# Differential attention: the four 32-row score products of two heads put into four PSUM banks

## The chip, the cores and the metric

The kernel runs on one core of a Trainium2 chip. The metric is the device time of one execution in microseconds (us): TensorE (PE) does the matrix products, VectorE (DVE) and ScalarE (ACT) the elementwise work, GpSimd (POOL) a little of it, and SyncE (SP) issues the weight loads.

## The reference, cut to what matters

Two layers of one transformer block are followed by two layers of another, over 512 tokens of width 1024. The second block's mixer has three attentions; the change lies in the first of these, differential attention with four heads of two 32-wide maps each:

```python
def diff_attention(q, k, v, lam):
    ...
        s = jnp.einsum('bhmqd,bhmkd->bhmqk', qblk, k).astype(jnp.float32) * scale
        qpos = bi * Q_BLOCK + jnp.arange(Q_BLOCK)
        s = jnp.where(kpos[None, :] <= qpos[:, None], s, -jnp.inf)
        p = jax.nn.softmax(s, axis=-1)
        a = p[:, :, 0] - lam * p[:, :, 1]
        return jnp.einsum('bhqk,bhkd->bhqd', a, vf)
```

Its output goes through a norm over each head's 64 values and, beside the outputs of the two other attentions, into the product with `w_out`.

## The kernel before

Every large product is split into three passes (`mm3`, L176 to L178) into one PSUM bank of tag `ps_mm`, of which there are three; a bank is free again when its reader has taken it. A weight comes by SP into a `wr` buffer, ACT casts it into a high part (L136, `wh`) and DVE subtracts that for the low part (L137, `wl`).

`mixers2` writes the second block's mixer in this order: forgetting attention; projections for differential attention; differential attention for the query tiles t = 3, 2, 1, 0 (at t, scores are 128 x 128(t+1) wide); projections `w_b2` with rotary embedding (`rope_proj`: three DVE operations L1064 to L1066, an addition on POOL L1067, transposes L1081, an ACT copy L1082) and `w_bv2`; then `to_feat` of the differential output (transposes L517), the dilated attention, and the product with `w_oa2`, whose first three of five input tiles come from the forgetting attention and whose last two from the differential one.

No one lays the instructions out by hand: `TileContext` with its scheduler sets the order on each engine, so products of a later line fill the time in which an earlier line's chain runs on DVE and ACT. Within an engine the order is then fixed, and an instruction that waits holds all behind it.

In differential attention one head goes like this. `score_pair` issues its two 32-row products into the two banks of tag `ps_S` (L1089; a 32-row product takes a quarter of the array's rows, and the first of a pair waits for the last read of the pair before, `sread`). `softmax_pair` takes each out with scale, mask and row minimum (DVE L1103) and exponentiates it (ACT L1105). Then the two maps are combined (DVE L1236 to L1240), and `pv` transposes the result in 128-wide pieces into one of the two banks of tag `ps_T` (L1115), copies it to SBUF (ACT L1117) and multiplies it with the values into `ps_o` (L1119). After four heads the tile is scaled (L1243), squared (L1246), summed (L1248), passed through a reciprocal root of eleven small DVE operations (L121 to L132) and scaled again (L1253). The dilated attention uses the same `softmax_pair` with 64-row products, two at a time.

Of the kernel before, what the change touches and what calls it, by code (L numbers as in the profile page):

```python
# [9 lines left out]
F32 = mybir.dt.float32  # L10
# [51 lines left out]
class Builder:  # L62
    def __init__(self, ctx, tc, d, out, cfg=None):
# [9 lines left out]
        self.pend, self.nstart, self.sread = [], 0, None  # L73
# [1010 lines left out]
    def score_pair(self, qk, ws):  # L1084

        nc = self.nc
        pts = [self.ps("S")[:, :ws] for _ in range(2)]
        for u, (q, k, row) in enumerate(qk):
            i = nc.tensor.matmul(pts[u], q, k, start=True, stop=True, tile_position=None if row is None else (row, 0))  # L1089
            if not u and self.sread is not None:  # L1090
                self.tc.add_manual_dep(i.ins, self.sread.name, SYNC, reason="pair")
        return pts

    def softmax_pair(self, mp, qk, t, in1s, scale):
# [5 lines left out]
        for pt, in1 in zip(pts, in1s):  # L1100
            s = mp.tile([P, S], F32, name="at_s", tag="at_s", bufs=5)[:, :w]
            st = mp.tile([P, 2], F32, name="at_st", tag="at_st", bufs=8)
            i = nc.vector.tensor_tensor_reduce(s, pt, in1, -scale, 3.0e38, ALU.add, ALU.min, accum_out=st[:, 0:1])  # L1103
            self.sread = i.ins
            nc.scalar.activation(s, s, AF.Exp, bias=st[:, 0:1], scale=-1.0, accum_out=st[:, 1:2])  # L1105
            out.append((s, st[:, 1:2]))
        return out

    def pv(self, mp, s, t, po, v):
# [7 lines left out]
        nc.scalar.copy(pT, tp[:, :w])  # L1117
# [39 lines left out]
    def mixers2(self, l, mp, act, nxt):  # L1157
# [69 lines left out]
        for t in reversed(range(NT)):  # L1227
# [3 lines left out]
            for h in range(4):  # L1231
                qt, kt = qka[h // 2], qka[2 + h // 2]
                rows = ((h % 2) * 64, (h % 2) * 64 + 32)
                (s0, d0), (s1, d1) = self.softmax_pair(mp, [(qt[b:b + 32], kt[b:b + 32], b) for b in rows], t, (msk, msk),
                                                       32 ** -0.5)
                nc.vector.reciprocal(den[:, h:h + 1], d0)  # L1236
                c = mp.tile([P, 1], F32, name="df_c", tag="df_c", bufs=4)
                nc.vector.reciprocal(c, d1)
                nc.vector.scalar_tensor_tensor(c, c, d0, lam[:, 2:3], ALU.mult, ALU.mult)
                nc.vector.scalar_tensor_tensor(s0, s1, c, s0, ALU.mult, ALU.add)  # L1240
                self.pv(mp, s0, t, po[:, h * 64:h * 64 + 64], lambda c: ya[c][:, h * 64:h * 64 + 64])
# [324 lines left out]
```

## Time and profile before

| | |
|---|---|
| time, median of 3 runs | 2783.43 us (2779.05 to 2784.21) |
| the profiled execution's own time | 2781.03 us |
| its span, first to last instruction | 2779.3 us |
| TensorE (PE) busy | 2701.2 us, 97% of the span |
| VectorE (DVE) busy | 1776.4 us, 64% |
| ScalarE (ACT) busy | 1181.6 us, 43% |
| chain that ended last | PE 77%, DVE 8%, DMA 8% |

The share of busy time is that of the whole span. The profile's chain runs back from the last instruction to what released each step. The two differential attentions lie at 1559 to 1632 us and 2230 to 2302 us of the span.

### The profile page before, as it was taken

To read this page: it belongs to the slowest core of one execution; us is meant where nothing else is said; L and a number is where in the kernel's file an instruction comes from. 1 tells how busy PE (TensorE), PEld (TensorE's weight loads), DVE (VectorE), ACT (ScalarE), POOL (GpSimd) and SP (SyncE) were. 2 spreads that over 40 slices of the span, in tenths; PEclk is the share of its full clock that TensorE was granted. 3 is DMA by queue.
4 is the path that set the end of the run, shared out by engine and by line. 5 is a ranking of instruction groups with operands and counts; after the bars stand their busy time and mean duration, and the time that the engine had idled before them with its cause. 6 is when DMAs were issued, how large, how long until landed. Compare 5 with 4: busy or idle time off the path is not lost.

```text
span 2779.3 us, 42737 instructions
## 1 busy us (share of the span) xinstructions
PE 2701.2 (97%) x16360; PEld 2305.9 (83%) x16360; DVE 1776.4 (64%) x3872; ACT 1181.6 (43%) x2340; POOL 250.6 (9%) x622
## 2 busy tenths in 40 slices
PE   8999999999999999999998999999999999999998
PEld 7887887889988788878987787888889787888887
DVE  7677777468676867765863666655554485664555
ACT  4644532326374543233543545333234554532332
POOL 2000100002200010000223200000001410100000
PEclk9999999999999999999999999999999999999999
DMA  4211487332221127743223221223332312133222
GB/s 155 75 41 62 131 267 230 107 106 92 88 75 44 59 82 245 257 151 106 99 72 104 52 68 65 83 89 97 102 94 86 99 39 84 49 105 97 89 86 78
DMA packets 87644, 285.59 MB, mean 103 GB/s; under 512 B 10972, under 2 KB 15132, under 8 KB 87440
## 3 DMA queue, kind: packets, MB, share of 16 engines
q1 hardware_dynamic: 81280, 266.49, 29.5%
q0 software_dynamic: 5872, 16.35, 2.2%
q8 instruction: 128, 2.10, 0.3%
q14 instruction: 76, 0.62, 0.1%
q10 hardware_dynamic: 288, 0.03, 0.0%
HBM read 280.69 MB, written 2.14 MB: 102 GB/s over the span
## 4 chain that ended last, share of the span: by engine, by line
PE 77%; DVE 8%; DMA 8%; ACT 3%; issue 2%; POOL 2%; SPq 0%; DVEq 0%; POOLq 0%; ACTq 0%
PE ps_mm L176 12%; PE ps_mm L177 12%; PE ps_mm L178 12%; DMA wm<-w_mod 6%; PE ps_T L176 5%; PE ps_T L178 5%; PE ps_T L177 5%; PE ps_S L176 5%; PE ps_S L178 5%; PE ps_S L177 5%; PE ps_S L1089 2%; DVE wm L1032 2%; PE ps_o L1135 1%; PE ps_T L1129 1%; PE ps_S L581 1%
## 5 line engine op out<-in xcount | busy, mean ns | idle before, releaser
L136 ACT CAST wh<-wr 128x1024 fp32r<-128x1024 f32 (+4 forms) x414 | 407.4, 987 | 677.4 <-PE ps_mm L177 225.8
L137 DVE TENSOR_TENSOR wl<-wr,wh 128x1024 fp32r<-128x1024 f32 (+4 forms) x414 | 472.5, 1142 | 305.0 <-ACT wh L136 297.8
L177 PE MATMUL ps_mm<-slotA,wh 128*128 128x512 f32 (+1 forms) x632 | 227.1, 362 | 3.4 <-DVE slotA L317 2.0
L176 PE MATMUL ps_mm<-slotA,wh 128*128 128x512 f32 (+1 forms) x632 | 226.2, 363 | 1.5 <-ACT slotA L316 0.7
L178 PE MATMUL ps_mm<-slotA,wl 128*128 128x512 f32 (+1 forms) x632 | 226.0, 359 | 0.0
L176 PE MATMUL ps_mm<-wh,slotA 128*128 128x256 f32 (+3 forms) x688 | 208.8, 304 | 0.0
L178 PE MATMUL ps_mm<-wh,slotA 128*128 128x256 f32 (+3 forms) x688 | 205.4, 299 | 0.0
L177 PE MATMUL ps_mm<-wl,slotA 128*128 128x256 f32 (+3 forms) x688 | 205.3, 299 | 0.0
L136 ACT CAST m_h<-tmp 128x512 fp32r<-128x512 f32 (+1 forms) x122 | 71.4, 587 | 209.2 <-DVE tmp L911 172.1
L1032 DVE CUSTOM_DVE_ANT_0 wm<-wm,sc 128x1024 f32<-128x1024 f32 x96 | 117.5, 1224 | 65.3 <-DMA wm<-w_mod 64.5
L176 PE MATMUL ps_mm<-slotB,wh 128*128 128x512 f32 (+1 forms) x408 | 142.5, 355 | 4.4 <-ACT slotB L136 3.6
L177 PE MATMUL ps_mm<-slotB,wh 128*128 128x512 f32 (+1 forms) x408 | 142.6, 350 | 1.4 <-DVE slotB L137 1.4
L176 PEld LDWEIGHTS ps_mm<-wh,slotA 128*128 128x128 f32 x688 | 131.6, 192 | 13.5 <-issue 10.6
L178 PE MATMUL ps_mm<-slotB,wl 128*128 128x512 f32 (+1 forms) x408 | 141.1, 346 | 0.0
L177 PEld LDWEIGHTS ps_mm<-slotA,wh 128*128 128x128 f32 x632 | 122.3, 194 | 22.3 <-DVE slotA L317 2.8
L176 PEld LDWEIGHTS ps_mm<-slotA,wh 128*128 128x128 f32 x632 | 121.3, 194 | 21.2 <-issue 3.0
L178 PEld LDWEIGHTS ps_mm<-slotA,wl 128*128 128x128 f32 x632 | 122.3, 193 | 18.2 <-issue 3.0
L178 PEld LDWEIGHTS ps_mm<-wh,slotA 128*128 128x128 f32 x688 | 131.2, 191 | 7.3 <-issue 6.6
L177 PEld LDWEIGHTS ps_mm<-wl,slotA 128*128 128x128 f32 x688 | 131.6, 191 | 5.2 <-issue 4.3
L176 PE MATMUL ps_S<-m_h,wh 128*128 128x512 f32 (+1 forms) x355 | 129.5, 365 | 3.2 <-DVE yacc L945 2.9
L178 PE MATMUL ps_S<-m_h,wl 128*128 128x512 f32 (+1 forms) x355 | 129.2, 364 | 0.0
L177 PE MATMUL ps_S<-m_l,wh 128*128 128x512 f32 (+1 forms) x355 | 129.2, 364 | 0.0
(635 smaller groups left out, 7177.4 us busy)
## 6 DMA issues: line engine op xcount, KB each, us to landing
wr<-w_up SPq DMA_DIRECT2D x152, 512.0 KB, 3.8
wm<-w_mod SPq DMA_DIRECT2D x96, 512.0 KB, 4.6
wr<-w_dn SPq DMA_DIRECT2D x64, 512.0 KB, 3.9
wr<-w_dn SPq DMA_DIRECT2D x32, 384.0 KB, 3.1
wr<-w_dn SPq DMA_DIRECT2D x32, 320.0 KB, 2.9
wr<-w_f SPq DMA_DIRECT2D x16, 512.0 KB, 3.8
wr<-w_pg SPq DMA_DIRECT2D x16, 512.0 KB, 3.7
wr<-w_t SPq DMA_DIRECT2D x12, 512.0 KB, 4.6
```

What stands on the lines that cost most here:

```text
L136: nc.scalar.copy(hi, src)
L137: nc.vector.tensor_tensor(lo, src, hi.bitcast(F32), ALU.subtract)
L176: nc.tensor.matmul(out, ah, bh, start=i == 0, stop=False)
L177: nc.tensor.matmul(out, ah, bl, start=False, stop=False)
L178: nc.tensor.matmul(out, al, bh, start=False, stop=i == n - 1)
L581: nc.tensor.matmul(pt, qs[f][b:b + 64, tt], qs[4][b:b + 64, k0:k0 + w], start=True, stop=True)
L1032: nc.vector.tensor_tensor_reduce(w, w, self.sc, 1.0, 0.0, ALU.mult, ALU.add, accum_out=self.mod[l][:, j:j + 1])
L1089: i = nc.tensor.matmul(pts[u], q, k, start=True, stop=True, tile_position=None if row is None else (row, 0))
L1129: nc.tensor.transpose(tp[:, c * P:c * P + P], s[:, c * P:c * P + P], self.ident)
L1135: nc.tensor.matmul(po[u * 64:u * 64 + 64], v(c, u), pT[:, c * P:c * P + P], start=c == 0, stop=c == t, tile_position=(0, u * 64))
```

## The change

The scores of two heads are asked for together: two products into the banks of `ps_S`, two into those of `ps_T`. The first of the four waits for the last reads of both kinds of bank (`sread`, and the new `tread`: the last eviction of a score from a `ps_T` bank or the last copy of transposed weights out of one). All four maps are then evicted and exponentiated, both heads are combined, and only then do the two heads' transposes and products with the values follow, written one after the other. Where a pair alone is asked for (the two other attentions), nothing changes.

```diff
     def score_pair(self, qk, ws):
...
-        pts = [self.ps("S")[:, :ws] for _ in range(2)]
+        pts = [self.ps(b)[:, :ws] for b in "SSTT"[:len(qk)]]
+        first = self.sread, self.tread if len(qk) > 2 else None
         for u, (q, k, row) in enumerate(qk):
             i = nc.tensor.matmul(pts[u], q, k, start=True, stop=True, tile_position=None if row is None else (row, 0))
-            if not u and self.sread is not None:
-                self.tc.add_manual_dep(i.ins, self.sread.name, SYNC, reason="pair")
+            for r in () if u else first:
+                if r is not None:
+                    self.tc.add_manual_dep(i.ins, r.name, SYNC, reason="pair")
         return pts
...
-            self.sread = i.ins
+            if n < 2:
+                self.sread = i.ins
+            else:
+                self.tread = i.ins
...
-        nc.scalar.copy(pT, tp[:, :w])
+        self.tread = nc.scalar.copy(pT, tp[:, :w]).ins
...
-            for h in range(4):
-                qt, kt = qka[h // 2], qka[2 + h // 2]
-                rows = ((h % 2) * 64, (h % 2) * 64 + 32)
-                (s0, d0), (s1, d1) = self.softmax_pair(mp, [(qt[b:b + 32], kt[b:b + 32], b) for b in rows], t, (msk, msk),
-                                                       32 ** -0.5)
...
-                self.pv(mp, s0, t, po[:, h * 64:h * 64 + 64], lambda c: ya[c][:, h * 64:h * 64 + 64])
+            for i in range(2):
+                qt, kt = qka[i], qka[2 + i]
+                four = self.softmax_pair(mp, [(qt[b:b + 32], kt[b:b + 32], b) for b in range(0, P, 32)], t, (msk,) * 4, 32 ** -0.5)
+                for h in (2 * i, 2 * i + 1):
+                    (s0, d0), (s1, d1) = four[h % 2 * 2:h % 2 * 2 + 2]
...
+                for h in (2 * i, 2 * i + 1):
+                    s0 = four[h % 2 * 2][0]
+                    self.pv(mp, s0, t, po[:, h * 64:h * 64 + 64], lambda c: ya[c][:, h * 64:h * 64 + 64])
```

The scheduler then lays out the instructions anew. On SP and POOL the order stays; on PE, DVE and ACT it differs in one stretch of each of the two layers, the same in both, and nowhere else. Every product that was there is there. In what follows `ps_S_15585` and the like are single banks' contents, and the line numbers of the changed kernel are 1 to 7 higher than those of the profile (L1090 is L1089, L1110 is L1105, L1120 is L1115, L1122 is L1117, L1124 is L1119, L1245 is L1240).

**First place: PE and ACT at t = 3, second half of the heads.** Before, the two products of a head (`ps_S`) stand together between passes of a `w_b2` projection:

```order
L176 MATMUL ps_mm_16107<-wh_16041,slotA_13688 128x256
L177 MATMUL ps_mm_16107<-wl_16042,slotA_13688 128x256
L1089 MATMUL ps_S_15585<-slotB_15103,slotB_15101 128x512
L1089 MATMUL ps_S_15586<-slotB_15103,slotB_15101 128x512
L178 MATMUL ps_mm_16107<-wh_16041,slotA_13689 128x256
```

Now one of the two `ps_T` products stands alone, right behind the transposes of the heads before (this stretch of PE's order), and the three others follow later, behind those heads' last product with the values (the next stretch):

```order
L1124 MATMUL ps_o_15527<-ya3_15403,at_pT_15568 128x64
L1120 MATMUL ps_T_15574<-ident_81,at_s_15545 128x128 x4
L1090 MATMUL ps_T_15587<-slotB_15103,slotB_15101 128x512
L176 MATMUL ps_mm_16193<-wh_16183,slotA_13680 128x256
L177 MATMUL ps_mm_16193<-wl_16184,slotA_13680 128x256
```

```order
L1124 MATMUL ps_o_15527<-ya3_15403,at_pT_15579 128x64
L1090 MATMUL ps_S_15585<-slotB_15103,slotB_15101 128x512
L1090 MATMUL ps_S_15586<-slotB_15103,slotB_15101 128x512
L1090 MATMUL ps_T_15588<-slotB_15103,slotB_15101 128x512
L1081 MATMUL ps_mm_16169<-ident_81,rp_a_16163 128x128
L1081 MATMUL ps_mm_16175<-ident_81,rp_a_16163 128x128
L176 MATMUL ps_mm_16193<-wh_16189,slotA_13692 128x256
```

The two products L1081 are the last transposes into two of the three `ps_mm` banks; six passes into the third follow, and the next pass needs the bank of `ps_mm_16169`. On ACT the copy that frees it (`slotB_16027`) stands, in the changed kernel, behind two of the four exponentials:

```order
L1122 COPY at_pT_15579<-ps_T_15574 128x512
L1110 ACTIVATE at_s_15593,at_st_15594<-at_s_15593,at_st_15594 128x512
L1110 ACTIVATE at_s_15597,at_st_15598<-at_s_15597,at_st_15598 128x512
L1082 COPY slotB_16027<-ps_mm_16169 128x512
L1082 COPY slotB_16028<-ps_mm_16175 128x512
L1110 ACTIVATE at_s_15601,at_st_15602<-at_s_15601,at_st_15602 128x512
L1110 ACTIVATE at_s_15605,at_st_15606<-at_s_15605,at_st_15606 128x512
```

What moved: the fourth product left the other three, and exponentials of 512 columns now stand ahead of the copy just after their scores were issued.

**Second place: DVE at t = 2, first half of the heads.** The names are `df_t`, `df_r` (the reciprocal root of the tile before), `rp_a`, `rp_b` (rotary embedding), `wl` (a weight's low part), `at_s` (the combined map). Before, the combination of the last head of that half stands so:

```order
L1064 TENSOR_TENSOR rp_a_16218<-ps_mm_16193,c_ropeb_14050 128x256
L1065 TENSOR_TENSOR rp_b_16219<-ps_mm_16193,c_ropeb_14050 128x4x32
L131 TENSOR_TENSOR df_t_15648<-df_t_15648,df_v_15647 128x4
L1066 TENSOR_TENSOR rp_b_16219<-ps_mm_16193,c_ropeb_14050 128x4x32
L1238 RECIPROCAL df_c_15731<-at_st_15727 128x1
L132 SCALAR_TENSOR_TENSOR df_r_15646<-df_t_15648,df_r_15646 128x4
L1239 SCALAR_TENSOR_TENSOR df_c_15731<-df_c_15731,at_st_15723,lam_15520 128x1
L130 TENSOR_TENSOR df_t_15648<-df_r_15646 128x4
L1240 SCALAR_TENSOR_TENSOR at_s_15722<-at_s_15726,df_c_15731,at_s_15722 128x384
```

Now a weight's low part of 768 columns stands just ahead of the combined map, and the rest of the rotary step behind it:

```order
L1243 RECIPROCAL df_c_15691<-at_st_15679 128x1
L130 TENSOR_TENSOR df_t_15648<-df_r_15646 128x4
L1244 SCALAR_TENSOR_TENSOR df_c_15691<-df_c_15691,at_st_15675,lam_15520 128x1
L1064 TENSOR_TENSOR rp_a_16311<-ps_mm_16286,c_ropeb_14050 128x256
L131 TENSOR_TENSOR df_t_15648<-df_t_15648,df_v_15647 128x4
L137 TENSOR_TENSOR wl_16484<-wr_16481,wh_16483 128x768
L1245 SCALAR_TENSOR_TENSOR at_s_15674<-at_s_15678,df_c_15691,at_s_15674 128x384
L1065 TENSOR_TENSOR rp_b_16312<-ps_mm_16286,c_ropeb_14050 128x4x32
L1066 TENSOR_TENSOR rp_b_16312<-ps_mm_16286,c_ropeb_14050 128x4x32
```

On PE the transposes of `at_s_15674` stand behind 14 passes of 256 columns and six L1081 that follow that group's scores; the next pass needs the bank `ps_mm_16286`, which the last of these rows frees.

**Third place: PE at the end, t = 0.** Before, passes of `w_bv2` stand around the last product with the values; 49 of them lie between it and the transposes L517 of the finished output:

```order
L177 MATMUL ps_mm_16531<-wl_16502,slotA_13694 128x384
L1119 MATMUL ps_o_15914<-ya0_15400,at_pT_16001 128x64
L178 MATMUL ps_mm_16531<-wh_16501,slotA_13695 128x384
L176 MATMUL ps_mm_16557<-wh_16483,slotA_13680 128x384
L177 MATMUL ps_mm_16557<-wl_16484,slotA_13680 128x384
```

Now these passes have all gone before, and so have 27 passes of `w_oa2` (nine into each of the three `ps_mm` banks, all that need no differential output); 16 of the 27 stand behind the scores of the first half of the heads at t = 0, and from there on no pass stands before L517. The order ends so (`ps_S_16663` and later are dilated attention):

```order
L1090 MATMUL ps_T_15963<-slotB_15103,slotB_15101 128x128
L1090 MATMUL ps_S_16663<-slotB_16030,slotB_16027 128x128
L1090 MATMUL ps_S_16664<-slotB_16030,slotB_16027 128x128
L1120 MATMUL ps_T_15994<-ident_81,at_s_15968 128x128
L1090 MATMUL ps_S_16687<-slotB_16031,slotB_16028 128x128
L1090 MATMUL ps_S_16688<-slotB_16031,slotB_16028 128x128
L1120 MATMUL ps_T_15999<-ident_81,at_s_15976 128x128
L1124 MATMUL ps_o_15914<-ya0_15400,at_pT_15996 128x64
L1090 MATMUL ps_S_16711<-slotB_16032,slotB_16029 128x128
L1090 MATMUL ps_S_16712<-slotB_16032,slotB_16029 128x128
L1124 MATMUL ps_o_15914<-ya0_15400,at_pT_16001 128x64
L517 MATMUL ps_T_16639<-ident_81,ya0_15400 128x128
```

What moved: the filler is spent before the last heads' chain begins, and the first three dilated score pairs moved into it.

## Rows read from the trace of the kernel before

**Rows 1.** The page's head: the span, then busy time, share of the span and instructions of each engine.
```profile
span 2779.3 us, 42737 instructions
PE 2701.2 (97%) x16360; PEld 2305.9 (83%) x16360; DVE 1776.4 (64%) x3872; ACT 1181.6 (43%) x2340; POOL 250.6 (9%) x622
```
**Rows 2.** Busy time by stretch, differential attention of the first and of the second layer of the block: from:to, length, then busy time (and instructions) of PE, PE's weight loads, DVE, ACT, POOL, the granted clock, DMA share and GB/s.
```profile
1559.00:1611.00 52.00, 52.00 (x392) 42.96 (x392) 43.22 (x167) 28.87 (x77) 8.30 (x10) 1.00 0.14 39
1611.00:1640.00 29.00, 29.00 (x201) 27.94 (x200) 18.14 (x88) 12.28 (x44) 2.75 (x3) 1.00 0.08 23
2230.00:2290.00 60.00, 60.00 (x462) 51.15 (x462) 51.01 (x210) 32.37 (x89) 9.63 (x11) 1.00 0.10 28
```
**Rows 3.** PE in order of time, four short stretches: start, length, engine, line, operation. A product counts as two instructions here, so x4 is a pair and x2 a single one. The last stretch is a single 64-row product of the dilated attention.
```profile
1568.34 0.28 PE L176 MATMUL ps_mm<-wh,slotA 128*128 128x256 f32 x1
1568.46 0.28 PE L177 MATMUL ps_mm<-wl,slotA 128*128 128x256 f32 x1
1568.67 1.13 PE L1089 MATMUL ps_S<-slotB 32*128 32x512 f32 x4
1569.73 0.38 PE L178 MATMUL ps_mm<-wh,slotA 128*128 128x256 f32 x1
...
1584.80 0.91 PE L1089 MATMUL ps_S<-slotB 32*128 32x384 f32 x4
1585.64 0.39 PE L177 MATMUL ps_mm<-wl,slotA 128*128 128x256 f32 x1
...
1600.38 0.70 PE L1089 MATMUL ps_S<-slotB 32*128 32x256 f32 x4
1601.02 0.39 PE L176 MATMUL ps_mm<-wh,slotA 128*128 128x256 f32 x1
...
1654.64 0.70 PE L1089 MATMUL ps_S<-slotB 64*128 64x256 f32 x2
1655.26 0.50 PE L178 MATMUL ps_mm<-slotA,wl 128*128 128x512 f32 x1
```
**Rows 4.** Groups of equal instructions between 1559 and 1640 us: busy us, mean ns of one, then the idle time before them and what ended it.
```profile
L1103 DVE CUSTOM_DVE_ANT_0 at_s<-ps_S,c_caus 128x384 f32<-128x384 f32 x8 | 4.3, 549 | 0.4 <-PE ps_S L1089 0.4
L1239 DVE SCALAR_TENSOR_TENSOR df_c<-df_c,at_st,lam 128x1 f32<-128x1 f32 x16 | 5.7, 354 | 0.3
L1064 DVE TENSOR_TENSOR rp_a<-ps_mm,c_ropeb 128x256 f32<-128x256 f32 x12 | 5.0, 416 | 0.0
L137 DVE TENSOR_TENSOR wl<-wr,wh 128x768 fp32r<-128x768 f32 x4 | 3.8, 950 | 0.0
L1082 ACT COPY slotB<-ps_mm 128x512 f32<-128x512 f32 x6 | 3.2, 589 | 2.6 <-PE ps_mm L1081 2.4
L1240 DVE SCALAR_TENSOR_TENSOR at_s<-at_s,df_c 128x384 f32<-128x384 f32 x4 | 2.5, 617 | 0.1
L131 DVE TENSOR_TENSOR df_t<-df_t,df_v 128x4 f32<-128x4 f32 x12 | 1.9, 156 | 0.2
L1243 DVE TENSOR_TENSOR ya<-ps_o,df_den 128x256 f32<-128x256 f32 x4 | 1.7, 422 | 8.3 <-PE ps_o L1119 8.3
L1248 DVE TENSOR_REDUCE df_ssq<-tmp 128x4 f32<-128x256 f32 x4 | 1.7, 416 | 0.6 <-ACT tmp L1246 0.6
```
**Rows 5.** ACT in order of time behind the first pair of scores at t = 3, which PE issues at 1559.51; in brackets the idle time before and what ended it.
```profile
1561.40 0.72 ACT L1105 ACTIVATE at_s<-at_s,at_st 128x512 f32<-128x512 f32 x1 [2.78 <-DVE at_st L1103]
1562.12 0.71 ACT L1105 ACTIVATE at_s<-at_s,at_st 128x512 f32<-128x512 f32 x1
1562.83 0.41 ACT L1131 COPY at_pT<-ps_T 128x128 f32<-128x128 f32 x2
```
**Rows 6.** From a pair of scores of t = 0 on PE to its combined map on DVE, in order of time (rows of both engines' timelines).
```profile
1613.10 0.49 PE L1089 MATMUL ps_S<-slotB 32*128 32x128 f32 x4
...
1615.97 0.35 DVE L1240 SCALAR_TENSOR_TENSOR at_s<-at_s,df_c 128x128 f32<-128x128 f32 x1
```
**Rows 7.** The end of differential attention, from DVE's, PE's and ACT's timelines: scaling of tile t = 0, its last scaling (four instructions), the transposes of the finished output, and their cast.
```profile
1631.95 0.42 DVE L1243 TENSOR_TENSOR ya<-ps_o,df_den 128x256 f32<-128x256 f32 x1 [6.92 <-PE ps_o L1119]
...
1635.64 0.87 DVE L1253 SCALAR_TENSOR_TENSOR ya<-ya,df_r,row 128x64 f32<-128x64 f32 x4
...
1640.34 1.04 PE L517 MATMUL ps_T<-ident,ya 128*128 128x128 f32 x8
...
1641.41 0.58 ACT L136 CAST slotA<-ps_T 128x512 fp32r<-128x512 f32 x1
...
1642.06 0.39 PE L177 MATMUL ps_mm<-slotA,wh 128*128 128x512 f32 x1
1642.29 0.39 PE L178 MATMUL ps_mm<-slotA,wl 128*128 128x512 f32 x1
```
**Rows 8.** PE's timeline where it had waited (in brackets how long), and busy time by stretch behind those waits, with the granted clock third from the end (columns as in rows 2).
```profile
1503.31 1.23 PE L1089 MATMUL ps_S<-slotB 64*128 64x512 f32 x2 [5.50 <-DVE at_st L1103]
...
1742.27 1.14 PE L266 MATMUL ps_mm<-n_dg,ones 128*128 128x256 f32 x2 [1.83 <-ACT n_dg L263]
...
1500.00:1507.00 7.00, 3.69 (x13) 2.18 (x14) 3.63 (x12) 3.01 (x8) 4.07 (x8) 0.51 0.42 150
...
1742.30:1745.80 3.50, 3.50 (x15) 3.32 (x16) 2.48 (x8) 2.02 (x5) 0.00 (x0) 0.51 0.01 2
```

More of the change, by code (lines that the diff above doesn't have):

```diff
@@ L72, in __init__ @@
         self.nmm, self.banks, self.late = 0, ("mm",), None
-        self.pend, self.nstart, self.sread = [], 0, None
+        self.pend, self.nstart, self.sread, self.tread = [], 0, None, None
         xa = cp.tile([P, NF * S], F32, name="x")
@@ L1099, in softmax_pair @@
         out = []
-        for pt, in1 in zip(pts, in1s):
+        for n, (pt, in1) in enumerate(zip(pts, in1s)):
             s = mp.tile([P, S], F32, name="at_s", tag="at_s", bufs=5)[:, :w]
@@ L1230, in mixers2 @@
             msk = self.c_caus[:, (3 - t) * P:]
-            for h in range(4):
-                qt, kt = qka[h // 2], qka[2 + h // 2]
-                rows = ((h % 2) * 64, (h % 2) * 64 + 32)
-                (s0, d0), (s1, d1) = self.softmax_pair(mp, [(qt[b:b + 32], kt[b:b + 32], b) for b in rows], t, (msk, msk),
-                                                       32 ** -0.5)
[L1236 to L1240, printed above, removed]
-                self.pv(mp, s0, t, po[:, h * 64:h * 64 + 64], lambda c: ya[c][:, h * 64:h * 64 + 64])
+            for i in range(2):
[3 more added lines that the diff above has]
+                    (s0, d0), (s1, d1) = four[h % 2 * 2:h % 2 * 2 + 2]
+                    nc.vector.reciprocal(den[:, h:h + 1], d0)
+                    c = mp.tile([P, 1], F32, name="df_c", tag="df_c", bufs=4)
+                    nc.vector.reciprocal(c, d1)
+                    nc.vector.scalar_tensor_tensor(c, c, d0, lam[:, 2:3], ALU.mult, ALU.mult)
+                    nc.vector.scalar_tensor_tensor(s0, s1, c, s0, ALU.mult, ALU.add)
+                for h in (2 * i, 2 * i + 1):
+                    s0 = four[h % 2 * 2][0]
+                    self.pv(mp, s0, t, po[:, h * 64:h * 64 + 64], lambda c: ya[c][:, h * 64:h * 64 + 64])
             o3 = ya[t].rearrange("p (h e) -> p h e", e=64)
```

## The prediction

> **What bounds the kernel now.** I began with the page's head: PE is busy in 97% of the span [rows 1], so a microsecond in which PE has nothing to do is probably a microsecond of the result. Then the busy time of the two stretches that the change reorders: PE is busy in all of 52.00 us, of 29.00 us and of 60.00 us, at the full clock, while DVE has 43.22 us of the first 52 [rows 2]. In this stage PE never waits; its filler, the passes of the next projections, covers every chain on DVE and ACT. So the change can gain only what it takes from PE's own work, and it loses whatever it uncovers. Last I read single instructions at the places where the order moved.
>
> **PE's own work.** From the start of a pair of 512-wide scores to the next instruction PE takes 1569.73 - 1568.67 = 1.06 us; at 384 it is 0.84, at 256 it is 0.64 [rows 3]. A single 64-row product of 256 columns takes 1655.26 - 1654.64 = 0.62 us [rows 3], as much as a pair: two products in different rows of the array run side by side, and one alone saves nothing. I call each such burst a unit. Before there are 16 units per layer. Four products issued together would make 8. But the new order does not issue four together. The third product waits only for its own `ps_T` bank, which comes free early; so it goes alone, and the three others follow, as the first place shows. That is again two units for two heads, and three for the first half at t = 3 (pair, one, one): 17 units, +1.06 us per layer. Against that, four fewer changes between passes and attention work (about 0.1 us each: between the pass at 1568.46 and the scores at 1568.67 lie 0.21 us instead of the 0.12 us between two passes [rows 3]) and one dilated unit of 0.62 us less, because its two products now stand together. I take **0** for PE's work. What three side by side cost no row shows; bounds are a pair (nothing more) and a pair and one more unit. I take the pair, because a pair costs the same as one.
>
> By the Trainium skill (TensorEngine Tiling (Array Packing), section Theoretical Speedup) a contraction of 32 rows or fewer can run up to four times as fast in row tiles. The pair rows agree for two, and no run here shows four; by it the 16 units would become 8, which is the second rival below.
>
> **The waits that the new order makes.** Two heads' chain is now one: four evictions, four exponentials, two combinations, and no next scores until the transposed copies have left the `ps_T` banks. I went through PE's order behind each group of scores and compared when PE arrives with when DVE and ACT are done. At most groups PE still arrives later. Three places are left in each layer.
>
> *First place (t = 3).* Behind the three scores PE has 1.06 us of scores, about 0.2 of transposes and six passes of 0.12 us [rows 3], so with changes of work it stands after 2.1 us before a pass whose bank is freed by the ACT copy. That copy comes behind two exponentials. Counted from the issue of the scores at 1559.51, the first exponential starts at 1561.40 and ACT is free for the next thing at 1562.83, 3.32 us later [rows 5]; with 0.59 us for the copy [rows 4] the bank is free at 3.9. **1.8 us.** Bounds: 0, since today such copies hold PE nowhere in this stage, and 2.5, if DVE is half a microsecond late with the evictions.
>
> *Second place (t = 2).* Scores 0.84, 14 passes of 0.12, six transposes of about 0.11 and changes of work: PE arrives after 3.35 us. DVE has from the same moment: scaling 0.42, four evictions of 0.55, sum 0.42, the rotary product 0.42, the weight's low part 0.95, the combination 0.35 and 0.62 and six small operations of about 0.16 [rows 4], together 6.3 us without a wait of its own. No filler is left, since two `ps_mm` banks wait for transposes and the third for the rotary step behind the combination. **3.0 us**; bounds 1.5 (means overlap by a tenth where operations follow each other) and 4.
>
> *Third place (the end).* After its scores for the first half at t = 0 PE has 16 passes of 512 columns, 0.23 us apart [rows 7], then only attention. From the end of those passes: transposes, copies and products of the first half until the last scores are issued, 1.5 us. From scores to a combined map a pair takes 1615.97 + 0.35 - 1613.10 = 3.2 us [rows 6]; the second combination adds 0.7, so 3.9. Transposes, a copy queued behind dilated exponentials, the product, and dilated work on DVE ahead of the scaling: 2.2. From scaling to the last scaling 1635.64 + 0.87 - 1631.95 = 4.6 us [rows 7], which today lies under the 8.4 us of passes up to L517 at 1640.34. Half the transposes and the cast of 0.58 us [rows 7]: 1.0. Together 13.2 us. In that time PE does some 4.0 us that it owes anyway (five units of 0.4, two of them the last scores, three dilated ones; eight transposes L517 of 1.0; the rest small). **9.2 us.** Bounds: 7, without the dilated work in between, and 12.
>
> *The clock.* After a wait of 5.50 us ended at 1503.31 the granted clock of the next microseconds was 0.51, the lower of its two levels (1.2 instead of 2.4 GHz); a wait of 1.83 us that ended at 1742.27 was followed by 3.50 us at 0.51 with PE busy throughout [rows 8]. Half speed for 3.5 us costs about 1.7 us. I take two such stretches per layer, behind the second and the third place: **3.4 us.** Bounds: one (1.7) and three (5.1).
>
> **The sum.** 1.8 + 3.0 + 9.2 + 3.4 + 0 = 17.4 us per layer, 34.8 for both. Against the profiled execution's own time: 2781.03 + 34.8 = 2815.8. That execution lies 2.4 us under the median of the runs shown, so I give **2818 us**. What follows the stage does not give it back: the passes spent early are the filler that is missing there later, and PE's total is the same.
>
> **The rivals.**
> 1. *Only the end waits* (slower, less). If DVE and ACT run further ahead of PE in the middle than my sums say, as they do today, the first two places vanish: 9.2 + 1.7 = 10.9, for two layers 21.8, about 2805; with the lower bound of the end 17.4, about 2801. For it: no wait of PE today in 141 us of this stage [rows 2]. Against: the bank at the second place is freed by an operation that stands behind 6 us of DVE work.
> 2. *Packing pays* (faster). If the lone product still runs beside its neighbours, or the four do meet, 8 units per layer fall away: 2 x (1.06 + 0.84 + 0.64 + 0.42) = 5.9 us, 11.8 for both layers, and if nothing waits the time is 2772. It decides at the moment the `ps_T` bank of the third product comes free: it would have to be no earlier than that of the fourth. Against it: in the order, transposes, products with the values or passes stand between the third and the other three in every group.
> 3. *Three do not pack.* If the third in a burst takes its own unit, seven bursts per layer add 1.06 + 2 x (0.84 + 0.64 + 0.42) = 4.9 us, 9.8 in all: 2828. For it: no row shows three. Against: one 64-row product costs what two cost.
> 4. *Nothing changes*: filler covers everything as today; then PE's work alone counts, 2781 to 2785. For it speaks the stage's record without a wait; against it the passes missing before L517.
>
> Another rule of the Trainium skill, on the same page (section PSUM Bottleneck), says that row packing speeds up TensorE but not the eviction of its banks. Had four met, the evictions behind them would still be what they are today, and the time would be that of the forecast less what rival 2 gains on PE; 43.22 us of DVE in 52 agree that there is little room.
>
> **How the numbers follow.** Forecast 0.56, rival 1 0.22, rival 3 0.12, rival 4 0.06, rival 2 0.04. The low end is rival 1 with the end at its lower bound, 2801, and I put it at 2800; the high end takes the upper bounds of the waits in both layers (12 + 4 + 2.5 + 5.1 = 23.6, 47.2 in all, 2831) or rival 3, and a little of both: 2836. A measurement of this kernel tells about 0.2% (5.6 us) from no change. Faster by more: rival 2, 0.04. Within: rival 4, 0.06. Slower by more: the rest, 0.90.
>
> **What would show it.** In the profile after, PE's row of the two stretches should fall under 100%: its timeline should show a wait at L176 ended by an ACT copy L1082 at t = 3, a wait at the transposes L1120 at t = 2 ended by DVE, and before L517 gaps that add up to some 9 us per layer, with a granted clock of 0.5 behind them. The scores should show as one product alone and three together, the three taking no longer than a pair. The forecast is wrong if PE stays busy in both stretches; if bursts of four appear; or if the waits are there and the time is not, because later waits shrank by as much.

## The result and the profile after

| | before | after |
|---|---|---|
| median of the runs | 2783.82 us (4 runs, 2779.05 to 2788.0) | 2820.38 us (4 runs, 2813.03 to 2823.0) |
| ratio | | 1.0133, 95% interval 1.0116 to 1.0149: slower by 1.2 to 1.5% |
| profiled execution, its span | 2781.03 us, 2779.3 us | 2818.74 us, 2817.0 us |

The forecast was 2818 us. Two of plan1's eleven executions took over 4000 us at a mean granted clock under 0.6 and are left out of its time below.

The head of the page after (span, then busy time and instructions of each engine), against [rows 1]:

```profile
span 2817.0 us, 42733 instructions
PE 2715.1 (96%) x16360; PEld 2313.3 (82%) x16360; DVE 1775.2 (63%) x3872; ACT 1180.3 (42%) x2340; POOL 250.3 (9%) x622
```

The span is 37.7 us longer, with 13.9 us more of busy PE although no product was added. To put both on a stage, I cut the trace at two products that stand in either kernel ahead of the second block's mixer and behind it (L266, which spreads a norm's factors), with the same 2048 instructions of PE between them. The two stretches before, one per layer (columns as in [rows 2]):

```profile
1440.98:1742.27 301.29, 289.71 (x2050) 243.25 (x2048) 173.71 (x559) 149.77 (x377) 54.39 (x106) 0.99 0.24 71
2110.81:2414.69 303.88, 290.96 (x2051) 245.50 (x2050) 172.86 (x556) 149.82 (x377) 54.34 (x106) 0.98 0.24 71
```

The same two after, then the five stretches of them in which the granted clock was at its lower level and was not before, then one stretch that was so before too:

```profile
1445.29:1763.69 318.40, 296.89 (x2051) 248.47 (x2049) 173.07 (x559) 149.40 (x377) 54.36 (x106) 0.97 0.23 68
2130.75:2452.82 322.07, 298.76 (x2050) 250.83 (x2049) 171.98 (x556) 149.16 (x377) 54.39 (x106) 0.95 0.22 67
...
1605.90:1609.30 3.40, 3.40 (x16) 3.40 (x17) 3.30 (x14) 0.58 (x2) 1.48 (x1) 0.50 0.66 175
1660.50:1670.70 10.20, 6.04 (x25) 4.62 (x26) 6.52 (x34) 3.87 (x15) 0.00 (x0) 0.50 0.00 0
2274.90:2278.30 3.40, 3.40 (x19) 3.40 (x18) 1.96 (x6) 0.67 (x2) 0.31 (x1) 0.50 0.02 5
2292.00:2295.40 3.40, 3.40 (x17) 3.36 (x16) 3.26 (x13) 0.48 (x1) 1.51 (x1) 0.50 0.72 209
2346.60:2356.80 10.20, 6.02 (x24) 4.74 (x25) 6.43 (x34) 3.76 (x13) 0.00 (x0) 0.50 0.00 0
...
1506.90:1513.70 6.80, 6.20 (x24) 4.69 (x25) 3.24 (x13) 3.55 (x9) 4.02 (x8) 0.50 0.44 134
```

The stage is 17.1 us longer in the first layer and 18.2 us in the second, 35.3 of the 37.7 us; the rest lies in unchanged code. Of these, length less busy PE, that is waiting, grew by 9.9 and 10.4 us, and busy PE by 7.2 and 7.8 us. Half of the busy time at 0.50 is what the clock cost: (3.40 + 6.04) / 2 = 4.7 and (3.40 + 3.40 + 6.02) / 2 = 6.4 us.

The largest of PE's waits after, between 1555 and 1672 us, where before there were none [rows 2]; the second layer has the same (us in total, times, longest):

```profile
PE ps_T L517 <- DVE ya L1260: 4.1, 1, 4.1
PE ps_T L1120 <- DVE at_s L1245: 3.3, 2, 2.2
PE ps_mm L176 <- ACT slotB L1082: 1.7, 1, 1.7
```

**First place.** PE's timeline at t = 3 after (a product counts as two instructions, so the first stretch is one product alone and the second three), to be held against [rows 3], and ACT's behind the same scores:

```profile
1581.35 1.12 PE L1090 MATMUL ps_T<-slotB 32*128 32x512 f32 x2
1582.40 0.38 PE L176 MATMUL ps_mm<-wh,slotA 128*128 128x256 f32 x1
...
1585.58 0.70 PE L1090 MATMUL ps_S<-slotB 32*128 32x512 f32 x2
1585.60 0.69 PE L1090 MATMUL ps_T<-slotB 32*128 32x512 f32 x1
1586.12 0.59 PE L1090 MATMUL ps_S<-slotB 32*128 32x512 f32 x2
1586.13 0.59 PE L1090 MATMUL ps_T<-slotB 32*128 32x512 f32 x1
1586.65 0.44 PE L1081 MATMUL ps_mm<-ident,rp_a 128*128 128x128 f32 x2
...
1589.52 0.39 PE L176 MATMUL ps_mm<-wh,slotA 128*128 128x256 f32 x1 [1.72 <-ACT slotB L1082]
```

```profile
1587.48 0.72 ACT L1110 ACTIVATE at_s<-at_s,at_st 128x512 f32<-128x512 f32 x1 [5.38 <-DVE at_st L1105]
...
1588.90 1.05 ACT L1082 COPY slotB<-ps_mm 128x512 f32<-128x512 f32 x2
```

The lone product takes 1582.40 - 1581.35 = 1.05 us, the three together 1586.65 - 1585.58 = 1.07: each a unit, like the pair of [rows 3]. Then PE stands 1.72 us before the bank whose copy ACT does behind two exponentials.

**Second place.** The scores at t = 2 and the transposes that wait, on PE, and on DVE the weight's low part ahead of the combined map:

```profile
1600.23 0.59 PE L1090 MATMUL ps_S<-slotB 32*128 32x384 f32 x2
...
1605.90 0.90 PE L1120 MATMUL ps_T<-ident,at_s 128*128 128x128 f32 x3 [2.23 <-DVE at_s L1245]
```

```profile
1604.37 0.95 DVE L137 TENSOR_TENSOR wl<-wr,wh 128x768 fp32r<-128x768 f32 x1
1605.23 0.61 DVE L1245 SCALAR_TENSOR_TENSOR at_s<-at_s,df_c 128x384 f32<-128x384 f32 x1
```

**Third place.** PE from the end of the passes (1655.95) to their resumption, and DVE's scaling and last scaling, against [rows 7]:

```profile
1655.95 0.38 PE L1120 MATMUL ps_T<-ident,at_s 128*128 128x128 f32 x2
...
1658.81 0.49 PE L1090 MATMUL ps_S<-slotB 64*128 64x128 f32 x4 [0.59 <-DVE at_st L1105]
1660.40 0.40 PE L1120 MATMUL ps_T<-ident,at_s 128*128 128x128 f32 x1 [1.10 <-DVE at_s L1245]
...
1663.03 0.69 PE L1124 MATMUL ps_o<-ya,at_pT 128*128 128x64 f32 x2
1667.83 1.97 PE L517 MATMUL ps_T<-ident,ya 128*128 128x128 f32 x8 [4.11 <-DVE ya L1260]
1669.62 1.49 PE L176 MATMUL ps_mm<-slotA,wh 128*128 128x512 f32 x3
```

```profile
1663.76 0.42 DVE L1250 TENSOR_TENSOR ya<-ps_o,df_den 128x256 f32<-128x256 f32 x1 [0.32 <-PE ps_o L1124]
...
1667.29 0.87 DVE L1260 SCALAR_TENSOR_TENSOR ya<-ya,df_r,row 128x64 f32<-128x64 f32 x4
```

From the end of the passes to the next pass are 1669.62 - 1655.95 = 13.7 us, the output's norm bare among them.

### The profile page after: what moved, and what is told of

The parts are those of the page before. It is cut to its first block, busy times and chain, and to the rows that moved or that the text cites. A ratio compares the mean times of both kernels' runs of the same rounds, so it can differ in the third digit from the quotient of the medians.

```text
span 2817.0 us, 42733 instructions
## 1 busy us (share of the span) xinstructions
PE 2715.1 (96%) x16360; PEld 2313.3 (82%) x16360; DVE 1775.2 (63%) x3872; ACT 1180.3 (42%) x2340; POOL 250.3 (9%) x622
## 4 chain that ended last, share of the span: by engine, by line
PE 76%; DVE 9%; DMA 8%; ACT 3%; issue 2%; POOL 2%; SPq 0%; DVEq 0%; POOLq 0%; ACTq 0%
PE ps_mm L176 12%; PE ps_mm L177 12%; PE ps_mm L178 12%; DMA wm<-w_mod 6%; PE ps_T L176 5%; PE ps_T L178 5%; PE ps_T L177 5%; PE ps_S L176 5%; PE ps_S L178 5%; PE ps_S L177 5%; PE ps_S L1090 2%; DVE wm L1032 2%; PE ps_o L1140 1%; DVE wl L137 1%; PE ps_T L1134 1%
## 5 line engine op out<-in xcount | busy, mean ns | idle before, releaser
L1110 ACT ACTIVATE at_s<-at_s,at_st 128x512 f32<-128x512 f32 (+3 forms) x160 | 89.1, 558 | 99.8 <-DVE at_st L1105 98.5
```

## The experiments

The changed kernel leaves open whether the chain of two heads is simply too long for the stage, or PE's order spends passes where the chip doesn't need them; and whether four products together would pay. How the kernels' stage stands (the two stretches of both layers together, cut as above; each number is the sum of two rows; waiting is length less busy):

| kernel | stage | PE busy | waiting | ratio to before, interval |
|---|---|---|---|---|
| before | 605.2 | 580.7 | 24.5 | |
| after | 640.5 | 595.7 | 44.8 | 1.0133 (1.0116 to 1.0149) |
| four_together | 641.2 | 589.8 | 51.4 | 1.0130 (1.0113 to 1.0147) |
| four_t32 | 639.0 | 596.7 | 42.2 | 1.0109 (1.0092 to 1.0125) |
| tog_t32 | 623.7 | 588.0 | 35.8 | 1.0057 (1.0042 to 1.0072) |
| hold_pv | 633.5 | 592.8 | 40.7 | 1.0098 (1.0083 to 1.0113) |
| plan3 | 609.2 | 581.4 | 27.7 | 1.0018 (1.0009 to 1.0027) |
| plan4 | 613.2 | 574.8 | 38.3 | 1.0031 (1.0019 to 1.0044) |
| plan7 | 611.7 | 573.5 | 38.3 | 1.0020 (1.0009 to 1.0031) |
| plan6 | 618.5 | 570.6 | 47.9 | 1.0046 (1.0030 to 1.0061) |
| plan1b | 607.4 | 572.0 | 35.5 | 1.0006 (0.9994 to 1.0018) |
| tog_t1 | 606.9 | 578.2 | 28.6 | 0.9985 (0.9974 to 0.9995) |
| plan8 | 600.8 | 568.9 | 31.9 | 0.9979 (0.9966 to 0.9992) |

Part of busy PE is work at the lower clock. I summed, over windows of 0.5 us, busy time times what the granted clock lacked to 1.00. Over both stretches this makes 6.3 us before, 18.7 after, 21.9 in four_together, 19.3 in four_t32, 18.6 in tog_t32, 6.5 in plan3 and 7.0 in plan8. Below I call this sum the clock.

One rewriting was not run because nothing would differ: with the products with the values written head by head inside the first loop, the order on every engine is that of the changed kernel. So the order does not hang on which of the two loops these lines stand in.

**four_together: all four products of a group wait alike**

```diff
-            for r in () if u else first:
+            for r in first if len(qk) > 2 or not u else ():
```

> The changed kernel, but each of a group's four products waits for the last reads of both kinds of bank, not only the first. PE's order then has three bursts for the first two heads at t = 3 (a pair, one, one) and seven bursts of four, where the changed kernel has 17 bursts per layer; so 10. Theory (a burst costs one unit however many row tiles it holds up to four, and the time is lost to waits behind it): a burst of four at 512 takes 1.06 us, and PE's work falls by 1.06 + 2 x (0.84 + 0.64 + 0.42) = 4.9 us per layer. If what PE saves stays saved, 2820 - 10 = 2810 us. If the chain of two heads on DVE and ACT is what bounds the end of the stage, what PE saves turns into waiting, and the time stays at 2816 to 2820 us with a longer wait before the finished output's transposes. Rival (four do not run side by side): a burst of four at 512 takes 2.1 us and the time stays near 2820 us without longer waits.

Measured: 2819.13 us. A burst of four at 512 takes 1582.38 - 1581.31 = 1.07 us, from its start to that of the next instruction. Busy PE fell by 5.9 us against the changed kernel, both layers together (9.7 expected; the clock took 3.2 us more), waiting rose by 6.6, and the stage is as long. The two largest of PE's waits in the first layer's stage:

```profile
PE ps_mm L176 <- ACT slotB L1082: 5.3, 2, 3.1
PE ps_T L517 <- DVE ya L1260: 4.1, 1, 4.1
```

What PE saves comes back as waiting, as the theory's second branch had it, but not at the end (4.1 us as before): behind the exponentials, where three now stand ahead of the copy (two in the changed kernel). So four do pack, and packing alone moves nothing.

**four_t32 and tog_t32: groups of four at t = 3 and 2 only**

```diff
+            for i in range(2) if t > 1 else ():
+                ...  # the group of four, as changed (tog_t32: with four_together's wait)
+            for h in () if t > 1 else range(4):
+                ...  # one head at a time, as before the change
```

> The changed kernel's groups of four at t = 3 and 2 only; t = 1 and 0 ask for pairs, head by head, as before the change. In PE's order no pass of a projection stands any more between the last product with the values and the transposes of the finished output, although t = 0 has no group of four. Theory (the end waits because the passes that covered it were spent earlier): the two waits of the middle stay (1.7 and 2.2 us), the end still waits some 4.5 us, the clock takes about 2 us, one lone product more 1.06: about 11 us per layer, 2783.8 + 22 = 2806 us. Rival (the end waits because of the two heads' common chain at t = 0): without groups of four there the end costs nothing, and the time is 2783.8 + 2 x (1.7 + 2.2 + 1.1) = 2794 us or less.

> Groups of four at t = 3 and 2 only, all four products of a group waiting for both kinds of bank; t = 1 and 0 ask for pairs, as before the change. PE's order has 14 bursts per layer in place of 16, and 48 passes between the last product with the values and the transposes of the finished output. Theory (a burst is one unit, and the loss is in the uncovered places): nothing waits at the end; PE's work is 2 x 0.84 = 1.7 us per layer less than before the change, and the wait at t = 3 behind the exponentials (1.7 us) may stay: 2780 to 2784 us. Rival (grouping two heads costs by itself, wherever it stands): half of the change's 36 us, about 2802 us.

Measured: four_t32 2811.84 us, tog_t32 2797.06 us. In four_t32 nothing at t = 0 is changed, and the end waits the same 4.11 us:

```profile
1658.43 1.97 PE L517 MATMUL ps_T<-ident,ya 128*128 128x128 f32 x8 [4.11 <-DVE ya L1271]
```

So it is the missing passes that lay the end bare, not the common chain at t = 0; four_t32's rival (2794 us) falls. In tog_t32 with its 48 passes L517 waits for nothing, as expected. But both times lie above the forecasts, by 6 and 13 us. In four_t32 busy PE grew by 8.0 us per layer, where I had 1.1 for a unit and 2 for the clock; the clock took 6.5. In tog_t32 the wait behind the exponentials is not 1.7 us but these two:

```profile
1584.31 0.58 PE L176 MATMUL ps_mm<-wh,slotA 128*128 128x256 f32 x1 [3.12 <-ACT slotB L1082]
...
1611.93 0.38 PE L176 MATMUL ps_mm<-wh,slotA 128*128 128x256 f32 x1 [1.43 <-ACT slotB L1082]
```

And in the first layer of tog_t32 the granted clock was at its lower level in these two stretches, where it was not before the change (columns as in [rows 2]):

```profile
1583.10:1589.90 6.80, 5.59 (x26) 5.60 (x27) 3.31 (x11) 2.35 (x6) 1.16 (x1) 0.50 0.00 0
1603.50:1606.90 3.40, 3.40 (x18) 3.40 (x17) 2.43 (x9) 0.00 (x0) 1.05 (x1) 0.51 0.57 186
```

Both layers together, tog_t32's stage is 18.5 us longer than before the change: waiting grew by 11.3 us and the clock by 12.3, and PE's other work fell by 5.0. My forecast had nothing for the clock. The time is nearer to tog_t32's rival (grouping costs by itself, about 2802 us) than to its theory, and this run alone does not refute that rival; plan3 and plan8 below, which group at every t, do.

**hold_pv: 27 passes moved to the end**

```diff
+        gate = self.tread    # behind the loop over t: the last copy of transposed maps
...
-            nc.tensor.matmul(out, ah, bh, start=i == 0, stop=False)
+            m = nc.tensor.matmul(out, ah, bh, start=i == 0, stop=False)
+            if not i and self.gate is not None:   # set around the products with w_oa2 alone
+                self.tc.add_manual_dep(m.ins, self.gate.name, SYNC, reason="gate")
```

> The changed kernel, but the first product into each bank for w_oa2 waits for the last transposed copy of differential attention, so the 27 passes that need no differential output stand behind the last product with the values, ahead of the transposes of the finished output. Theory (the stage is a chain of eight rounds that is longer than the passes can cover; filler moved to the end is missing earlier): the wait before the output's transposes (4.1 us) goes, a wait of some 2 us comes at t = 0 in front of the transposes of the first half's maps, since these maps were ready 0.9 to 1.6 us before PE came to them; about 2 us per layer less: 2815 us (2810 to 2820). Rival (only the place of the filler is at fault): the whole end wait with its clock comes back, 9 us per layer: 2802 us.

Measured: 2809.25 us, just past the theory's end of the range and well short of the rival's. The wait before L517 is gone; that before the transposes of the maps (L1123, after's L1120) is now the largest:

```profile
PE ps_T L1123 <- DVE at_s L1248: 6.4, 3, 3.3
PE ps_mm L177 <- ACT slotB L1085: 1.7, 1, 1.7
```

These passes came from t = 1 and 0, and what they cover at the end they leave bare there: of the 6.4 us, 2.2 are the second place's, as in the changed kernel, and 3.3 are one wait at t = 0, in front of the transposes. That fits either reason; the passes of the middle had still to be tried.

**plan3: the whole filler dosed by hand**

```diff
+            if not i and self.plan:   # the first pass into each bank, in program order
+                g = self.plan.pop(0)
+                if g is not None:
+                    self.tc.add_manual_dep(m.ins, self.rounds[g], SYNC, reason="plan")
...
+            self.rounds.append(i.ins.name)   # the last score product of a group of four
...
+        self.plan = [None, None, 0, 0, 1, 1, 2, 2, 3, 3, 4, 4, 5, 6, 7, 7, 7, 7, 7, 7, 7, 7, 7, 7]
```

(The list names, for twelve banks of `w_b2`, four of `w_bv2` and eight of `w_oa2`, the group that the first pass waits for.) Lines of the experiments stand up to 18 lower than in the changed kernel.

> The changed kernel with its filler dosed by hand: the first pass into each bank of the projections behind differential attention waits for the last score product of a stated group, at most two banks for each of the groups at t = 3, 2 and 1, one or two for t = 0, and the passes of w_oa2 for the last group. PE's order then has 41 passes behind the last transposes of differential attention and ahead of those of the finished output, where the changed kernel has none. The bursts stay 17 or so per layer. Theory (the order spends passes in the middle that the chip does not need there, so the end stands bare): the end wait of 6 us and most of the clock's 6 us per layer go, no wait over 3 us takes their place, and the time is 2783 + 2 x (1.1 for one more unit + 2 to 4 for waits of the middle) = 2790 us (2786 to 2800). Rival (the chain of eight groups is longer than all passes of the stage, wherever they stand): the waits come back in the middle and the time stays over 2808 us.

Measured: 2785.37 us, a little under the theory's range; the stage is 4.0 us longer than before the change where the changed kernel's is 35.3. All of PE's waits in the first layer's stage (L1127 are the maps' transposes, L1131 the products with the values):

```profile
PE ps_o L1131 <- ACT at_pT L1129: 0.9, 2, 0.5
PE ps_T L1127 <- DVE at_s L1253: 0.8, 1, 0.8
PE ps_mm L177 <- ACT slotA L137: 0.4, 1, 0.4
```

The same attention with the same grouping, and passes that come later: about nine tenths of the loss are gone. The chain is not longer than the passes; the scheduler's order had spent them too early. The rival falls. The clock is back at 6.5 us, too.

**plan1, plan4, plan7, plan6: eight bursts of four, with doses**

All have four_together's wait, count the other attentions' copies out of `ps_T` too (`self.tread = nc.scalar.copy(...)` in `pv2` and `out_scaled`), and differ in the list alone (- is None; last eight always 7):

| | `w_b2` | `w_bv2` |
|---|---|---|
| plan1 | 0 0 1 1 2 2 3 3 4 4 5 5 | 6 7 7 7 |
| plan4 | - 0 0 1 1 2 2 3 3 4 4 5 | 6 7 7 7 |
| plan7 | - - 0 0 1 1 1 2 2 3 3 4 | 4 5 6 7 |
| plan6 | 0 0 1 1 1 2 2 2 3 3 4 4 | 5 6 7 7 |
| plan8 | - - 0 0 1 1 2 2 3 3 4 4 | 5 6 7 7 |

> All four products of a group wait for both kinds of bank, the copies of the other attentions out of the ps_T banks count too, and the filler is dosed as in plan3, two banks per group. PE's order has eight bursts of four per layer and 48 passes behind the last product with the values. Theory (four products are one unit, and the loss is only in the uncovered places): PE's work falls by 5.9 us per layer against the kernel before the change; with waits of 2 to 4 us left in the middle: 2783 - 11.8 + 2 x 3 = 2777 us (2771 to 2785). Rival (the chain is longer than the passes): waits of 10 us per layer in the middle, 2795 us and more.

> As plan1, but the banks of the projections are dosed one group earlier by one bank (one before the first group, then two per group), so the transposes of the rotated projections fall elsewhere among the groups. Theory: as plan1, 2771 to 2785 us; where the two differ, the difference is the waits at the banks whose copies stand behind exponentials of 512 columns at t = 3, some 1.5 to 3 us each. Rival as for plan1.

> As plan1 and plan4 (eight bursts of four per layer, filler dosed), with two banks of the projections ahead of the first group, three for the second half at t = 3, and the w_bv2 banks one group earlier: 36 passes instead of 29 (plan4) between the first burst at t = 3 and the transposes, and 27 instead of 48 behind the last transposes. In plan4 the transposes at t = 3 were ready 5.3 us after the burst's start and PE came 0.5 us too early at each of four places. Theory (four products are one unit; what is left is filler a few passes short at each group): PE's work 5 us per layer less than before the change, waits of 3 to 5 us per layer (plan4: 6.7 to 7.1): 2775 to 2783 us. Rival (each group of four costs a fixed wait that filler cannot cover, because the banks of the projections are served by DVE and ACT behind the group's own work): 7 us of waits as in plan4, 2783 to 2788 us.

> As plan7 with the doses 2, 3, 3, 2, 2 for the groups at t = 3, 2 and 1 and one or two w_bv2 banks for t = 0: 19 passes stand between the first burst at t = 3 and its transposes and 42 behind the second. Theory: the first group is short by some 16 passes of 0.12 us (2 us of waiting), the second and third are covered; waits of 4 to 6 us per layer, 2777 to 2785 us. Rival (fixed wait per group): 2783 to 2788 us.

Measured: plan1 2783.64 us (ratio 1.0000, interval 0.9987 to 1.0014), plan4 2788.01, plan7 2787.43, plan6 2794.55 us. Busy PE in plan4, plan7 and plan6 is 5.8 to 10.1 us less than before the change, both layers together, and waiting 13.8 to 23.4 us more. plan1 lies at the upper end of its range, plan4 above its own, plan7 in the range of its rival (2783 to 2788 us), plan6 above theory and rival: how the doses meet the groups is worth more than the saving. In plan7, which put only 27 passes at the end, the output's transposes (now L522) wait again:

```profile
PE ps_T L522 <- DVE ya L1268: 1.9, 1, 1.9
```

**plan1b: plan1 once more**, for its profile

> The kernel of plan1 once more, because its profiled execution was a disturbed one. Theory: PE's work 5 to 6 us per layer less than before the change and 5 to 6 us of waits at the groups' transposes and at the banks of the projections, so that the time is that of the kernel before: 2778 to 2786 us. Rival: waits under 3 us per layer, 2775 us or less.

Measured: 2782.21 us, the time of the kernel before; busy PE 8.7 us less, waiting 11.0 us more, both layers together. Per layer that is 4.4 us of work, where the theory had 5 to 6, and 5.5 us of waits, as it had: what packing gives, waits take.

**plan8: the doses of plan3, with bursts of four**

> The doses of plan7 for the first three groups (two banks of the projections ahead of the first group, two for each of the next), but two banks, not three, for the second half at t = 3 and one group later for w_bv2, so that 43 passes instead of 27 stand behind the last transposes. Theory (a wait goes where passes are put in front of it): the 1.9 us before the finished output's transposes go, the other waits of plan7 (4.6 us in the first layer) stay at 4 to 5 us, PE's work stays 5 to 6 us per layer under the kernel before: 2777 to 2783 us, at most a whisker faster than before. Rival (the waits of the groups go up by what the end gets): 2783 to 2788 us, as plan7.

Measured: 2776.08 us, faster than before by 0.08 to 0.34% and just under the theory's range. PE's timeline at the first group and at the end:

```profile
1566.28 0.70 PE L1095 MATMUL ps_S<-slotB 32*128 32x512 f32 x2 [0.26 <-ACT tmp L1158]
1566.30 0.70 PE L1095 MATMUL ps_T<-slotB 32*128 32x512 f32 x2
1566.82 0.59 PE L1095 MATMUL ps_S<-slotB 32*128 32x512 f32 x2
1566.83 0.59 PE L1095 MATMUL ps_T<-slotB 32*128 32x512 f32 x2
1567.36 0.39 PE L177 MATMUL ps_mm<-wh,slotA 128*128 128x256 f32 x1
...
1648.10 1.09 PE L522 MATMUL ps_T<-ident,ya 128*128 128x128 f32 x8
```

Four products of 512 columns take 1567.36 - 1566.28 = 1.08 us, about what one takes, and the transposes of the output wait for nothing. Its two stretches:

```profile
1442.84:1741.92 299.08, 283.60 (x2050) 240.52 (x2049) 172.13 (x559) 149.67 (x377) 54.19 (x106) 0.99 0.24 72
2108.97:2410.66 301.69, 285.31 (x2050) 242.38 (x2049) 171.04 (x556) 149.76 (x377) 53.99 (x106) 0.98 0.24 71
```

Against plan3, whose list is the same but whose groups come in 16 bursts per layer, busy PE is 6.2 us less per layer; eight bursts fewer make 2 x (1.06 + 0.84 + 0.64 + 0.42) = 5.9. Against before the change, busy PE is 5.9 us less per layer and waiting 3.7 us more. That is half of the 7 us per layer that plan7's rival asked for (a fixed wait per group), so this rival falls, and so does plan8's own (2783 to 2788 us). It beats both kernels, by little: in one profiled execution each, the stage is 4.4 us shorter than before the change.

**tog_t1: groups of four at t = 1 only, nothing dosed**

> Groups of four at t = 1 only (two groups per layer), all four products waiting for both kinds of bank; t = 3, 2 and 0 ask for pairs as before the change; no dosing by hand. PE's order keeps 47 passes behind the last product with the values. Theory (a burst is one unit; a group of four saves one and is charged the waits that its own place leaves bare): PE's work 2 x 0.64 = 1.3 us per layer less than before the change, waits of 0.5 to 2 us per layer as in plan7's groups at t = 1: 2780 to 2785 us, no difference that can be told. Rival (nothing is bare where so much filler stands, so the saving is kept): 2780 us or a little under. Rival (grouping costs by itself): a quarter of the change's 36 us, 2792 us.

Measured: 2778.32 us, ratio 0.9985. The wait in the first layer's stage belongs to a group, and the end has none:

```profile
PE ps_mm L176 <- DVE df_den L1241: 1.4, 1, 1.4
```

Busy PE is 1.2 us per layer less and waiting 2.1 us more than before the change, near the theory's 1.3 and 0.5 to 2; the time is a little under its range and in that of the first rival (2780 us or a little under, the saving is kept), which the waits speak against. Since the stage of its profiled execution is 1.7 us longer than before the change, I don't call the 0.15% a gain of the groups; where it comes from stays open.

## Why the prediction was right, step by step

The forecast of 2818 us came out within 2.4 us of the median. Its terms per layer, and what the profile after shows in the first and the second:

| term | forecast | first layer | second layer |
|---|---|---|---|
| first place | 1.8 | 1.7 | 1.7 |
| second place | 3.0 | 2.2 | 2.2 |
| end | 9.2 | 6.0 | 6.0 |
| clock | 3.4 | 4.7 | 6.4 |
| PE's work and the rest | 0 | 2.5 | 1.9 |
| sum | 17.4 | 17.1 | 18.2 |

(End: 0.24 + 0.59 + 1.10 + 4.11 us. The last line is what is left of the stage's 17.1 and 18.2 us.)

**The sum is right partly by luck**: waits were put 4 us too high and the clock with PE's work 4 to 5 us too low. Part of that is booking. Of the 10.2 us at 0.50 some 9 lie inside the end, ahead of the next pass, and half of PE's 5.0 us of work there, 2.5 us, stands in the row of the clock, while the forecast had counted the whole end in one sum. Counted its way, the end cost 8.5 us, where 9.2 was forecast, and the clock elsewhere 2.2 and 4.0 us, where 3.4 was forecast. What luck is left: 1.6 us too much for the three places met some 2 us of work that had been put at nothing.

- *First place*: right in each part. PE came 1587.80 - 1585.58 = 2.2 us after the scores (forecast 2.1), the bank was free after 3.9 (forecast 3.9).
- *Second place*: the mechanism holds, the size was off. PE came after 3.4 us (forecast 3.35), but the combined map was done after 1605.84 - 1600.23 = 5.6 us and not 6.3: I had added the means of DVE's operations, and in the timeline each starts before the one ahead has ended (1604.37 + 0.95 is later than 1605.23). The bound of 1.5 named that; the value taken should have used it.
- *End*: from the last pass to the next were 13.7 us, forecast 13.2. Wrong was what PE does in it: 4.0 us by forecast, 13.67 - 6.04 = 7.6 by the trace, because 5.0 of it ran at 0.50 of the clock (at the full clock it would be 5.1). Work at half speed inside a wait for DVE only fills the wait. I had charged it under the clock as well as under the wait.
- *Clock*: two stretches of 3.5 us were forecast; the trace has two and three, and the one at the end lasts 10.2 us: it starts at 1660.50, behind three waits (0.24, 0.59 and 1.10 us) rather than one, and holds the fourth. My bound of three short stretches (5.1) was under the second layer's 6.4.
- *PE's work*: 0 was too low. One more unit is 1.06; in the first layer the stretch at 0.50 that was there before the change fell on more busy time (6.20 us of 6.80, where [rows 8] has 3.69 of 7.00), (6.20 - 3.69) / 2 = 1.3 us, which I put down to where the stretch fell, not to the change. In the second layer that stretch explains only 0.2 us, and some 0.7 of the 1.9 stay unexplained. The savings that I had set against the unit do not show.
- *Rivals*. Only the end waits: no, both middle places wait, to the tenth in both layers. Three do not pack: no, 1.07 us. Nothing changes: no. Packing pays: not in the changed kernel, which never issues four together; but plan8 shows that the price I gave for it, 5.9 us per layer, is right once the places are covered.

The rule of the Trainium skill that I set beside this (TensorEngine Tiling (Array Packing), section Theoretical Speedup: up to four times as fast where 32 rows or fewer are contracted) agrees with plan8, where four take 1.08 us and one in the changed kernel 1.05. Its section PSUM Bottleneck, that packing does not speed up the evictions, agrees as well: an eviction of 512 columns takes DVE 0.69 us before the change and in plan8, DVE is busy 346.6 and 343.2 us in the two stretches, and it is DVE's and ACT's work behind the scores that PE waits for.

What I had not seen is why the end was bare. I took the passes' early place as given. plan3 shows that it was a fault of the order and could be mended without touching the attention.

What stays open: why the scheduler, which had left 49 passes at the end before the change, spends them earlier here. In the changed kernel PE comes to the first transposes of the last group at t = 1 some 1.9 us after both maps are done (1644.98 against 1643.09 us), so there passes stand in front that the chip doesn't need; with the doses of plan4 the order puts transposes at t = 3 0.5 us too early. I did not try to tell these apart.

## What to carry to other kernels

Count units, not products: a burst of up to four 32-row products in separate row tiles takes about the time of one, so packing pays only if products really become ready together, and a wait that only the first of them has does not see to that. Where filler covers chains, look first at what stands behind the last link of the last chain; if nothing does, move filler there from places where PE comes late anyway, before anything else is changed. And charge a lower clock only to stretches in which PE would not have waited.

## What the runs showed of the hardware

- One, two, three and four 32-row products of 512 columns in different row tiles took 1.05, 1.06 [rows 3], 1.07 and 1.08 us.
- The same wait of 1.72 us at t = 3 did not have the same effect in both layers: behind it the clock stayed at its upper level in the first and was at 0.50 for 3.4 us in the second (2274.90), although PE's instructions are the same. Behind the wait of 2.23 us at t = 2 it was at 0.50 for 3.4 us in both.
- Three short waits in a row (0.24, 0.59 and 1.10 us), with little work between them, were followed by 10.2 us at 0.50 in both layers; a fourth wait of 4.11 us lies within these, and PE was busy for 6.0.
